# Attention scores of two heads in turn on the two halves of TensorE's rows, and forgetting-head values taken transposed on the halves of its columns

## The chip, the cores and the metric

One core of one Trainium2 chip. The metric is the device time of one execution in microseconds (us), of the slowest core, here the only one.

## The reference, cut to what matters

Two decoder layers over 256 tokens of width 1024, float32. Each has a token mixer, and after it a dense SwiGLU (layer 0) or a top-2-of-8 expert SwiGLU (layer 1); every sub-layer ends in a LayerNorm. The token mixer has two causal attention branches on one input projection:

```python
fq, fk, fv, fg, dq, dk, dv, ga, gb = jnp.split(u @ w_in, IN_SPLIT_POINTS, axis=-1)
# forgetting heads: 8 heads of 64, bias from a running sum of log-sigmoid gates
s = einsum('bqhd,bkhd->bhqk', fq, fk) * 64**-0.5 + cum_q - cum_k     # causal mask
y_fox = einsum('bhqk,bkhd->bqhd', softmax(s), fv)
# differential heads: 4 heads, two score maps each over 64, values of 128
s = einsum('bqhcd,bkhcd->bhcqk', dq, dk) * 64**-0.5 + rel_bias       # causal mask
p = softmax(s); a = p[:, :, 0] - lam * p[:, :, 1]
o = einsum('bhqk,bkhe->bqhe', a, dv)                                 # then an RMS norm per head
merged = sigmoid(ga) * (y_fox @ w_br_fox) + sigmoid(gb) * (y_diff @ w_br_diff)
mix = merged @ w_out
```

## The kernel before, in words

The queries lie in two blocks `t` of 128 tokens; block 0 sees 128 keys, block 1 sees 256 (`kw`). Large products run as pairs of reduced-precision parts (`whi`, `wlo` of a weight, `hTh`, `hTl` of the activations): `split` (L180 to L182) makes `whi` on ScalarE and `wlo` on VectorE from a loaded `raw`. Attention scores, transposes and values run in plain float32, for which TensorE makes two passes, each a weight load and a matmul.

`mixer` (L456 on) projects the forgetting values and gates, then `fq` and `fk`, and then runs two generators beside projections (`beside`, L506): `fox()`, the forgetting heads, beside the projections of `dk`, `dq` and `dv`; and `diff()`, the differential heads, beside those of the gates. The order of each engine's queue is not the order of the code: a scheduler puts the instructions in order when the program is built, by its own estimate of when each is ready.

`qk["fq"]` and its like hold two heads per 128-partition column block: the even head in partitions 0 to 63, the odd head in 64 to 127. A score product therefore contracts over 64 partitions and uses half of TensorE's rows.

`fox()` takes for each block the even heads, then the odd ones (`b`), in groups of four heads (block 0) or two (block 1). A group is one PSUM bank of tag `aux` (two buffers): the bias product `cum_RA,cum_L` and the mask product `maskb,identb` over all 128 rows, then one `fk,fq` product per head on half `b` of the rows; `softmax` (L435: one maximum on VectorE, one exponential per head on ScalarE); `blocks_T` (L448: four transposes, one copy by ScalarE); then per head and key block

```python
self.mm(o[:, h * 64:(h + 1) * 64], pT[:, blk * 128:(blk + 1) * 128],
        v["f", kb][:, h * 64:(h + 1) * 64], kb == 0, kb == t)
```

with tokens on `o`'s partitions: a weight load of 128 columns and a stream of 64. At the block's end VectorE divides `o` by the sums (L559), and `put_T` (L201) turns the result by four transposes and splits it into `yT`.

`diff()` has for each group the two maps `c` of a head in the two row halves; it does the bias products, the scores and the softmax of `c = 0` and then those of `c = 1`, normalises both on VectorE (L587, L588) and goes on as above, with values of 128 columns.

All matmuls are issued at L92 (`mm`). In the experts stage `plain_mm` (L977) already lets 2 or 4 products run on column halves or quarters of the array, one after the other by order-only dependencies; those are the products `aux<-raw,xs`.

Of the kernel before, what the change touches and what calls it, by code (L numbers as in the profile page):

```python
# [8 lines left out]
F32 = mybir.dt.float32  # L9
# [4 lines left out]
OP = mybir.AluOpType  # L14
# [43 lines left out]
class Body:  # L58
# [397 lines left out]
    def mixer(self, l, xT):  # L456
        nc, a, tc = self.nc, self.a, self.tc
        w = a["w_in"][l].rearrange("(k p) n -> p k n", p=128)
# [4 lines left out]
        v = {}  # L463
# [16 lines left out]
        qk = {}  # L480
# [36 lines left out]
        L, RA = self.forget(fg)  # L517
        yts = {}

        def y_tile():  # L520
            return self.at.tile([128, 512], F32, name="y", tag="y", bufs=2)

        def y_T(half):

            if half not in yts:
                yts[half] = [self.gran("yT", F32R) for _ in range(2)]
            return yts[half]

        def fox():
            for t in range(2):  # L530
                o = self.o_bank()
                si = self.at.tile([128, 8], F32, name="fsum", bufs=2)
                groups = [(b, 0, 4) for b in range(2)] if t == 0 else [(b, g, 2) for g in range(2) for b in range(2)]
                for b, g, n in groups:
                    heads = [b + 2 * (2 * g + i) for i in range(n)]
                    kw = 128 * (t + 1)
                    ps = self.aux_bank()
                    p3 = ps.rearrange("p (n w) -> p n w", w=kw)
                    h0 = heads[0]
                    self.mm(p3, L[:, t * 128:(t + 1) * 128], RA[b][:, 2 * g:2 * g + n, 0:kw], True, False)  # L540
                    self.mm(p3[:, :, kw - 128:kw], self.identb,
                            self.maskb[:, None, :].to_broadcast([128, n, 128]), False, False)
                    r0 = b * 64
                    for i in range(n):
                        jj = 2 * g + i
                        self.mm(p3[:, i], qk["fq"][r0:r0 + 64, jj, t * 128:(t + 1) * 128],
                                qk["fk"][r0:r0 + 64, jj, 0:kw], False, i == n - 1)
                    p, s = self.softmax(ps, n, kw, "p")
                    nc.vector.reciprocal(si[:, h0:h0 + 2 * n - 1:2], s[:, :n])
                    pT = self.blocks_T(p)  # L550
                    for i in range(n):
                        h = heads[i]
                        for kb in range(t + 1):
                            blk = i * (t + 1) + kb
                            self.mm(o[:, h * 64:(h + 1) * 64], pT[:, blk * 128:(blk + 1) * 128],
                                    v["f", kb][:, h * 64:(h + 1) * 64], kb == 0, kb == t)
                    yield
                yf = y_tile()
                nc.vector.tensor_tensor(yf.rearrange("p (h e) -> p h e", e=64),  # L559
                                        o.rearrange("p (h e) -> p h e", e=64),  # L560
                                        si[:, :, None].to_broadcast([128, 8, 64]), op=OP.mult)
                self.put_T(y_T(0), yf, t)

        def diff():
            for t in range(2):
                o = self.o_bank()
                kw = 128 * (t + 1)
                for g, n in ([(0, 4)] if t == 0 else [(0, 2), (2, 2)]):
                    pp = []
                    for c in range(2):  # L570
                        ps = self.aux_bank()
                        p3 = ps.rearrange("p (n w) -> p n w", w=kw)
                        for i, part in enumerate(self.bias):
                            self.mm(p3, self.antir, part[:, g:g + n, 256 - kw:256], i == 0, False)
                        for i in range(n):
                            self.mm(p3[:, i], qk["dq"][c * 64:c * 64 + 64, g + i, t * 128:(t + 1) * 128],
                                    qk["dk"][c * 64:c * 64 + 64, g + i, 0:kw], False, i == n - 1)
                        p, s = self.softmax(ps, n, kw, ("p", "p2")[c])
                        r = self.at.tile([128, 4], F32, name="sm_r", bufs=4)
                        nc.vector.reciprocal(r[:, :n], s[:, :n])  # L580
                        if c == 1:
                            nc.vector.tensor_scalar(r[:, :n], r[:, :n], lamn, None, op0=OP.mult)
                        pp.append((p, r))
                    (p1, r1), (p2, r2) = pp
                    for i in range(n):
                        cs = slice(i * kw, (i + 1) * kw)
                        nc.vector.tensor_scalar(p1[:, cs], p1[:, cs], r1[:, i:i + 1], None, op0=OP.mult)  # L587
                        nc.vector.scalar_tensor_tensor(p1[:, cs], p2[:, cs], r2[:, i:i + 1], p1[:, cs],  # L588
                                                       op0=OP.mult, op1=OP.add)
                    pT = self.blocks_T(p1)  # L590
                    for i in range(n):
                        h = g + i
                        for kb in range(t + 1):
                            blk = i * (t + 1) + kb
                            self.mm(o[:, h * 128:(h + 1) * 128], pT[:, blk * 128:(blk + 1) * 128],
                                    v["d", kb][:, h * 128:(h + 1) * 128], kb == 0, kb == t)
                    yield
                yd = y_tile()
                nc.scalar.activation(yd, o, AF.Square)
                ss = self.at.tile([128, 4], F32, name="ss", bufs=2)  # L600
                nc.vector.tensor_reduce(ss, yd.rearrange("p (h e) -> p h e", e=128), axis=AX, op=OP.add)
                nc.vector.tensor_scalar(ss, ss, 1.0 / 128.0, EPS, op0=OP.mult, op1=OP.add)
                rs = self.rsqrt(ss, 4)
                yd3 = yd.rearrange("p (h e) -> p h e", e=128)
                nc.vector.tensor_tensor(yd3, o.rearrange("p (h e) -> p h e", e=128),
                                        rs[:, :, None].to_broadcast([128, 4, 128]), op=OP.mult)
                nc.vector.tensor_tensor(yd3, yd3, sub[:, None, :].to_broadcast([128, 4, 128]), op=OP.mult)
                self.put_T(y_T(1), yd, t)
# [6 lines left out]
        def gating(i):  # L615
            for nm, c0 in (("a", C_GA), ("b", C_GB)):
# [5 lines left out]
                yield  # L622

        beside(fox(), (z for part in (proj("dk", C_DK, 1.0), proj("dq", C_DQ, 0.125), values()) for z in part), 0)
        beside(diff(), (z for i in range(4) for z in gating(i)), 0)

        if l == DEPTH - 1:
# [7 lines left out]
        for i in range(2):  # L635
            wpc = [self.piece(wb[j][:, :, 512 * i:512 * i + 512]) for j in range(2)]
            for jp in range(2):
                parts = []
                for br in range(2):
                    b = self.mm_bank()  # L640
                    for j in range(2):
# [3 lines left out]
                                                   op0=OP.add, op1=OP.mult)  # L645
# [3 lines left out]
                cs = slice(jp * 512, jp * 512 + 512)  # L649
                nc.scalar.activation(mt["h", i][:, cs], m, AF.Copy, scale=0.5)  # L650
                nc.vector.scalar_tensor_tensor(mt["l", i][:, cs], m, 0.5, mt["h", i][:, cs].bitcast(F32),
                                               op0=OP.mult, op1=OP.subtract)
# [786 lines left out]
```

## Time and profile before

| | |
|---|---|
| median of 3 runs | 1545.66 us (1544.31 to 1545.85) |
| profiled execution: its time, its span | 1546.93 us, 1545.2 us |
| TensorE busy (matmuls) | 1510.6 us, 98% |
| VectorE, ScalarE busy | 911.6 us (59%), 734.7 us (48%) |
| DMA, mean over the span | 294 GB/s |

Engines are named as in the profile: PE is TensorE's matmuls, PEld its weight loads, DVE VectorE, ACT ScalarE. A row of the order of time gives the start and the length of a group of equal instructions; a matmul's length takes in the time until its result has left the pipeline, so lengths of neighbours overlap, and the distance between starts tells what each costs the queue. A form such as `64*128 64x256` means a stationary operand of 64 rows and 128 columns and a moving one of 64 partitions and 256 columns.

### The profile page before, as it was taken

The numbers are of one execution on the slowest core, as the hardware profiler recorded it, in microseconds if no ns is written. First come the engines' busy times: TensorE is split into PE (matmuls) and PEld (weight loads), VectorE is DVE, ScalarE is ACT, GpSimd is POOL, SyncE is SP. The second block draws the span as 40 slices with busy tenths as digits, with TensorE's granted clock in tenths as the row PEclk, the third lists the DMA queues.
The fourth block names the chain that finished last, engine by engine and source line by source line (L and its number), as shares of the span: only waits on it lengthen the run. The fifth ranks groups of instructions, "written<-read, shape, count | busy, mean of one in ns | idle before, by whom it ended". The sixth has DMA issues, their size and how long they took to land. (4 is left out here: it accounts for less than half of the span.)

```text
span 1545.2 us, 24215 instructions
## 1 busy us (share of the span) xinstructions
PE 1510.6 (98%) x8798; PEld 1144.6 (74%) x8798; DVE 911.6 (59%) x1274; ACT 734.7 (48%) x1049; POOL 16.6 (1%) x43
## 2 busy tenths in 40 slices
PE   8999999999999999999999999999999999999996
PEld 6989979998798898666666566666666666666762
DVE  7546685545664657544535443766657576566774
ACT  4554444444365533254443333556555455555660
POOL 3000000000000000000000000000000000000000
PEclk9999999999999999999999999999999999999998
DMA  9633555555473340699999999999999999999993
GB/s 293 197 118 107 187 169 188 190 177 164 140 256 110 109 164 1 264 409 406 405 409 401 394 396 401 409 409 403 383 391 409 382 403 409 381 404 401 396 399 137
DMA packets 187347, 454.73 MB, mean 294 GB/s; under 512 B 13050, under 2 KB 68370, under 8 KB 187220
## 3 DMA queue, kind: packets, MB, share of 16 engines
q1 hardware_dynamic: 186432, 452.05, 77.9%
q0 software_dynamic: 784, 1.05, 0.5%
q8 instruction: 71, 1.16, 0.3%
q14 instruction: 56, 0.46, 0.1%
q10 hardware_dynamic: 4, 0.01, 0.0%
HBM read 452.00 MB, written 1.05 MB: 293 GB/s over the span
## 5 line engine op out<-in xcount | busy, mean ns | idle before, releaser
L182 DVE TENSOR_TENSOR wlo<-raw,whi 128x1024 fp32r<-128x1024 f32 (+2 forms) x524 | 617.2, 1202 | 370.1 <-ACT whi L181 365.4
L181 ACT ACTIVATE whi<-raw 128x1024 fp32r<-128x1024 f32 (+2 forms) x524 | 529.2, 1042 | 272.8 <-PE mm L92 168.6
L92 PE MATMUL mm<-hTh,wlo 128*128 128x256 f32 x672 | 192.2, 286 | 0.0
L92 PE MATMUL mm<-hTl,whi 128*128 128x256 f32 x672 | 191.8, 285 | 0.0
L92 PE MATMUL mm<-hTh,whi 128*128 128x256 f32 x672 | 191.1, 284 | 0.0
L92 PE MATMUL mm<-wlo,xh 128*128 128x512 f32 x448 | 179.8, 402 | 2.4 <-DVE wlo L182 2.0
L92 PE MATMUL mm<-whi,xl 128*128 128x512 f32 x448 | 175.1, 391 | 0.0
L92 PE MATMUL mm<-whi,eh 128*128 128x512 f32 x504 | 162.9, 398 | 0.6 <-ACT whi L181 0.6
L92 PE MATMUL aux<-raw,xs 128*32 128x512 f32 (+1 forms) x896 | 156.2, 598 | 0.0
L92 PE MATMUL mm<-whi,xh 128*128 128x512 f32 x448 | 154.6, 404 | 1.2 <-ACT whi L181 1.1
L92 PEld LDWEIGHTS mm<-hTh,wlo 128*128 128x128 f32 x672 | 128.5, 191 | 2.9 <-issue 2.0
L92 PEld LDWEIGHTS mm<-hTl,whi 128*128 128x128 f32 x672 | 128.7, 191 | 0.2
L92 PEld LDWEIGHTS mm<-hTh,whi 128*128 128x128 f32 x672 | 128.6, 191 | 0.2
L92 PEld LDWEIGHTS mm<-whi,eh 128*128 128x128 f32 x504 | 92.4, 188 | 38.0 <-ACT whi L181 9.6
L92 PEld LDWEIGHTS mm<-whi,xh 128*128 128x128 f32 x448 | 80.7, 188 | 46.7 <-issue 15.7
L92 PE MATMUL mm<-wlo,eh 128*128 128x512 f32 x280 | 107.9, 399 | 0.3
L92 PEld LDWEIGHTS mm<-wlo,xh 128*128 128x128 f32 x448 | 84.1, 188 | 25.4 <-DVE wlo L182 9.0
L92 PEld LDWEIGHTS aux<-raw,xs 128*32 128x32 f32 (+1 forms) x896 | 41.4, 123 | 82.0 <-issue 78.3
L1031 ACT ACTIVATE rows<-aux 128x512 f32<-128x512 f32 x56 | 33.3, 595 | 139.8 <-PE aux L92 139.8
L92 PEld LDWEIGHTS mm<-whi,xl 128*128 128x128 f32 x448 | 84.3, 188 | 16.8 <-issue 0.8
L92 PE MATMUL aux<-raw,eh 128*32 128x512 f32 (+1 forms) x448 | 78.7, 599 | 0.0
L92 PEld LDWEIGHTS mm<-wlo,eh 128*128 128x128 f32 x280 | 52.6, 188 | 12.1 <-DVE wlo L182 1.0
(323 smaller groups left out, 1976.4 us busy)
## 6 DMA issues: line engine op xcount, KB each, us to landing
raw<-in_w_expert_gate_up SPq DMA_DIRECT2D x448, 512.0 KB, 9.3
raw<-in_w_expert_down SPq DMA_DIRECT2D x224, 512.0 KB, 9.2
raw<-in_w_in SPq DMA_DIRECT2D x36, 1024.0 KB, 5.3
raw<-in_w_ffn_gate_up SPq DMA_DIRECT2D x22, 1024.0 KB, 5.0
raw<-in_w_ffn_down SPq DMA_DIRECT2D x10, 1024.0 KB, 4.9
raw<-in_w_out SPq DMA_DIRECT2D x8, 1024.0 KB, 5.0
raw<-in_w_in SPq DMA_DIRECT2D x8, 520.0 KB, 4.7
raw<-in_w_branch_fox SPq DMA_DIRECT2D x4, 1024.0 KB, 4.9
```

Source lines behind the costliest of these rows:

```text
L92: self.made = self.nc.tensor.matmul(out, lhsT, rhs, start=start, stop=stop)
L181: return (self.nc.scalar.activation(hi, src, AF.Copy), self.nc.vector.tensor_sub(lo, src, hi.bitcast(F32)))
L182: self.nc.vector.tensor_sub(lo, src, hi.bitcast(F32)))
L1031: self.nc.scalar.activation(r, bk, AF.Copy)
```

## The change

`fox()` and `diff()` now take both row halves of a group at once. A helper `in_turn` issues products that alternate between the two halves, each ordered behind the one before without a wait:

```diff
+        def in_turn(products):
+            made = []
+            for x in products:
+                self.mm(*x)
+                made.append(self.made.ins)
+            for x, y in zip(made, made[1:]):
+                self.behind(y, x, mybir.DependencyClass.NoSync)
```

In `fox()` the even and the odd heads of a group get a bank each, and both banks are filled before the softmax of either. The probabilities are divided by their sums on VectorE before they are transposed. The value product has its operands exchanged: the values (64 columns) are the stationary operand, the transposed probabilities (128 columns) stream, and the result is transposed already, with even heads on partitions 0 to 63 of `o` and odd heads on 64 to 127. So `o` is split straight into `yT`:

```diff
-                    self.mm(p3, L[:, t * 128:(t + 1) * 128], RA[b][:, 2 * g:2 * g + n, 0:kw], True, False)
...
-                    for i in range(n):
-                        jj = 2 * g + i
-                        self.mm(p3[:, i], qk["fq"][r0:r0 + 64, jj, t * 128:(t + 1) * 128],
-                                qk["fk"][r0:r0 + 64, jj, 0:kw], False, i == n - 1)
-                    p, s = self.softmax(ps, n, kw, "p")
-                    nc.vector.reciprocal(si[:, h0:h0 + 2 * n - 1:2], s[:, :n])
-                    pT = self.blocks_T(p)
...
-                nc.vector.tensor_tensor(yf.rearrange("p (h e) -> p h e", e=64),
-                                        o.rearrange("p (h e) -> p h e", e=64),
-                                        si[:, :, None].to_broadcast([128, 8, 64]), op=OP.mult)
-                self.put_T(y_T(0), yf, t)
+                    in_turn((p3[b][:, i], qk["fq"][rows[b], 2 * g + i, t * 128:(t + 1) * 128],
+                             qk["fk"][rows[b], 2 * g + i, 0:kw], False, i == n - 1) for i in range(n) for b in range(2))
+                    ps = []
+                    for b in range(2):
+                        p, s = self.softmax(p3[b].rearrange("p n w -> p (n w)"), n, kw, ("p", "p2")[b])
+                        r = self.at.tile([128, 4], F32, name="sm_r", bufs=4)
+                        nc.vector.reciprocal(r[:, :n], s[:, :n])
+                        for i in range(n):
+                            cs = slice(i * kw, (i + 1) * kw)
+                            nc.vector.tensor_scalar(p[:, cs], p[:, cs], r[:, i:i + 1], None, op0=OP.mult)
+                        ps.append(p)
                     yield
+                    pT = [self.blocks_T(p) for p in ps]
+                    in_turn((o[rows[b], (2 * g + i) * 128:(2 * g + i + 1) * 128],
+                             v["f", kb][:, (2 * (2 * g + i) + b) * 64:(2 * (2 * g + i) + b + 1) * 64],
+                             pT[b][:, (i * (t + 1) + kb) * 128:(i * (t + 1) + kb + 1) * 128], kb == 0, kb == t)
+                            for i in range(n) for kb in range(t + 1) for b in range(2))
+                    yield
+                cut = [p.rearrange("p (k s) -> p k s", s=256)[:, :, t * 128:(t + 1) * 128] for p in y_T(0)]
+                self.split(*cut, o.rearrange("p (k s) -> p k s", s=128))
```

In `diff()` the bias products of both maps come first, then the scores of all heads by `in_turn`, alternating between `c = 0` and `c = 1`, then both softmaxes; its values stay as they are.

Where the scheduler now puts the products: TensorE's queue at three places, the same in both layers. A row is one product of the code (two passes of the trace where it is float32), `x4` four in a row.

First, layer 0, block 0 of the forgetting heads. Before:

```order
L92 MATMUL aux<-cum_RA,cum_L 128x512
L92 LDWEIGHTS identb
L92 MATMUL aux<-maskb,identb 128x512
L92 MATMUL aux<-fk,fq 128x128 x4
L92 MATMUL mm<-hTh_157,whi 128x256
L92 MATMUL aux<-cum_RA,cum_L 128x512
L92 LDWEIGHTS identb
L92 MATMUL aux<-maskb,identb 128x512
L92 MATMUL aux<-fk,fq 128x128 x4
```

After the change:

```order
L92 MATMUL aux<-cum_RA,cum_L 128x512
L92 LDWEIGHTS identb
L92 MATMUL aux<-maskb,identb 128x512
L92 MATMUL aux<-fk,fq 128x128
L92 MATMUL mm<-hTh_157,whi 128x256
...
L92 MATMUL mm<-hTh_157,whi 128x256
L92 MATMUL aux<-cum_RA,cum_L 128x512
L92 LDWEIGHTS identb
L92 MATMUL aux<-maskb,identb 128x512
L92 MATMUL aux<-fk,fq 128x128 x7
```

The scheduler pulls the first even head ahead of the odd heads' bank, with seven projection matmuls between; the other seven products follow in one visit.

Second, layer 0, block 1 of the forgetting heads, the second group. Before, the two score visits and the values stand apart, of which this is the first score visit:

```order
L92 MATMUL aux<-cum_RA,cum_L 128x512
L92 LDWEIGHTS identb
L92 MATMUL aux<-maskb,identb 128x2x128
L92 MATMUL aux<-fk,fq 128x256 x2
L92 MATMUL mm<-whi,hTh_157 128x512
L92 MATMUL mm<-wlo,hTh_157 128x512
L92 MATMUL mm<-whi,hTl_159 128x512
L92 MATMUL mm<-whi,hTh_157 128x512
L92 MATMUL mm<-wlo,hTh_157 128x512
L92 MATMUL o<-fv,pT 128x64 x4
```

After the change:

```order
L92 MATMUL aux<-cum_RA,cum_L 128x512
L92 LDWEIGHTS identb
L92 MATMUL aux<-maskb,identb 128x2x128
L92 MATMUL aux<-cum_RA,cum_L 128x512
L92 LDWEIGHTS identb
L92 MATMUL aux<-maskb,identb 128x2x128
L92 MATMUL aux<-fk,fq 128x256 x2
L92 MATMUL o<-pT,fv 64x128 x7
L92 MATMUL aux<-fk,fq 128x256 x2
L92 MATMUL mm<-whi,hTh_157 128x512
```

Seven value products of the group before now stand inside the score visit; the eighth stands alone ahead of it.

Third, layer 0, block 0 of the differential heads. Before:

```order
L92 MATMUL aux<-bias_h,antir 128x512
L92 MATMUL aux<-bias_l,antir 128x512
L92 MATMUL aux<-dk,dq 128x128 x4
L92 MATMUL aux<-bias_h,antir 128x512
L92 MATMUL aux<-bias_l,antir 128x512
L92 MATMUL aux<-dk,dq 128x128 x4
L92 MATMUL mm<-hTh_157,wlo 128x256
```

After the change:

```order
L92 MATMUL aux<-bias_h,antir 128x512
L92 MATMUL aux<-bias_l,antir 128x512
L92 MATMUL aux<-bias_h,antir 128x512
L92 MATMUL aux<-bias_l,antir 128x512
L92 MATMUL aux<-dk,dq 128x128 x8
L92 MATMUL mm<-hTh_157,wlo 128x256
```

Two visits became one of eight products. Elsewhere in a layer the score products now come, in this order, as 1, 2 and 1 (block 1 of the forgetting heads, first group), as 2 and 2 (above), and as 1, 3 and 4 (block 1 of the differential heads); before they came as 1, 1, 1, 1, 2, 2 and 2, 2, 2, 2. The value products of the forgetting heads come as 1, 7, 1, 7 and 8. The queues of SyncE and GpSimd, which issue the DMAs, read the same in both kernels.

## Rows read from the trace of the kernel before

**Rows 1.** Stretches 66:140 and 463:537: us, busy by engine, PEclk, DMA share, GB/s

```profile
66.00:140.00 74.00, 74.00 (x497) 63.22 (x496) 38.63 (x78) 38.60 (x96) 0.00 (x0) 1.00 0.36 114
463.00:537.00 74.00, 74.00 (x496) 63.22 (x495) 38.71 (x77) 38.68 (x96) 0.21 (x1) 1.00 0.36 114
```

**Rows 2.** Order of time, PE, 66.6 to 68.4: start us, us, engine line op

```profile
66.68 0.39 PE L92 MATMUL aux<-maskb,identb 128*128 128x512 bf16 x1
67.00 1.16 PE L92 MATMUL aux<-fk,fq 64*128 64x128 f32 x8
...
68.31 0.40 PE L92 MATMUL aux<-cum_RA,cum_L 128*128 128x512 f32 x1
```

**Rows 3.** Order of time, PE, 93.0 to 96.9

```profile
93.09 0.28 PE L92 MATMUL aux<-maskb,identb 128*128 128x256 bf16 x1
93.31 1.13 PE L92 MATMUL aux<-fk,fq 64*128 64x256 f32 x4
...
94.95 0.40 PE L92 MATMUL mm<-whi,hTl 128*128 128x512 f32 x1
95.18 0.40 PE L92 MATMUL mm<-whi,hTh 128*128 128x512 f32 x1
...
95.65 1.00 PE L92 MATMUL o<-fv,pT 128*128 128x64 f32 x8
...
96.77 0.39 PE L92 MATMUL mm<-whi,hTh 128*128 128x512 f32 x1
```

**Rows 4.** Order of time, PE, 73.5 to 75.7

```profile
73.60 0.28 PE L92 MATMUL aux<-maskb,identb 128*128 128x256 bf16 x1
73.81 0.70 PE L92 MATMUL aux<-fk,fq 64*128 64x256 f32 x2
...
74.69 0.70 PE L92 MATMUL aux<-fk,fq 64*128 64x256 f32 x2
...
75.61 0.27 PE L451 MATMUL tp<-ident,p 128*128 128x128 f32 x1
```

**Rows 5.** Order of time, PE, 117.6 to 118.4

```profile
117.65 0.60 PE L205 MATMUL tp<-ident,y 128*128 128x128 f32 x4
...
118.21 0.28 PE L92 MATMUL mm<-hTh,wlo 128*128 128x256 f32 x1
118.33 0.28 PE L92 MATMUL mm<-hTh,whi 128*128 128x256 f32 x1
```

**Rows 6.** Order of time, PE and then PEld, 980 to 985 (experts, column halves)

```profile
980.24 3.65 PE L92 MATMUL aux<-raw,xs 128*64 128x512 f32 x16
983.83 1.20 PE L92 MATMUL tp<-y,back 128*128 128x512 f32 x4
984.87 0.40 PE L92 MATMUL mm<-whi,xh 128*128 128x512 f32 x1
...
980.24 0.20 PEld L92 LDWEIGHTS aux<-raw,xs 128*64 128x64 f32 x4 [0.37 <-PE tp L92]
980.73 0.14 PEld L92 LDWEIGHTS aux<-raw,xs 128*64 128x64 f32 x2 [0.29 <-issue]
981.15 0.14 PEld L92 LDWEIGHTS aux<-raw,xs 128*64 128x64 f32 x2 [0.29 <-issue]
981.58 0.14 PEld L92 LDWEIGHTS aux<-raw,xs 128*64 128x64 f32 x2 [0.29 <-issue]
```

**Rows 7.** Groups by line and form, 66 to 140: line engine op xcount | busy us, mean ns | idle

```profile
L440 DVE TENSOR_REDUCE sm_m<-aux 128x4 f32<-128x512 f32 x4 | 2.8, 692 | 3.6 <-PE aux L92 3.6
L587 DVE TENSOR_SCALAR p<-p,sm_r 128x256 f32<-128x256 f32 x4 | 1.2, 350 | 0.0
L587 DVE TENSOR_SCALAR p<-p,sm_r 128x128 f32<-128x128 f32 x4 | 0.9, 282 | 0.0
...
L444 ACT ACTIVATION_READ_ACCUMULATOR p<-aux,sm_m 128x1 f32 x32 | 6.4, 200 | 0.0
L444 ACT ACTIVATE p<-aux,sm_m 128x128 f32<-128x128 f32 x16 | 5.7, 366 | 3.5 <-DVE sm_m L440 3.1 <-issue 0.4
```

More of the change, by code (lines that the diff above doesn't have):

```diff
@@ L531, in fox @@
                 o = self.o_bank()
[L532 to L539, printed above, removed]
-                    self.mm(p3, L[:, t * 128:(t + 1) * 128], RA[b][:, 2 * g:2 * g + n, 0:kw], True, False)
-                    self.mm(p3[:, :, kw - 128:kw], self.identb,
-                            self.maskb[:, None, :].to_broadcast([128, n, 128]), False, False)
-                    r0 = b * 64
-                    for i in range(n):
-                        jj = 2 * g + i
-                        self.mm(p3[:, i], qk["fq"][r0:r0 + 64, jj, t * 128:(t + 1) * 128],
-                                qk["fk"][r0:r0 + 64, jj, 0:kw], False, i == n - 1)
-                    p, s = self.softmax(ps, n, kw, "p")
-                    nc.vector.reciprocal(si[:, h0:h0 + 2 * n - 1:2], s[:, :n])
-                    pT = self.blocks_T(p)
[L551 to L556, printed above, removed]
-                    yield
@@ L558, in fox @@
-                yf = y_tile()
-                nc.vector.tensor_tensor(yf.rearrange("p (h e) -> p h e", e=64),
-                                        o.rearrange("p (h e) -> p h e", e=64),
-                                        si[:, :, None].to_broadcast([128, 8, 64]), op=OP.mult)
-                self.put_T(y_T(0), yf, t)
+                kw = 128 * (t + 1)
+                n = 4 // (t + 1)
+                for g in range(t + 1):
+                    p3 = []
+                    for b in range(2):
+                        ps = self.aux_bank()
+                        p3.append(ps.rearrange("p (n w) -> p n w", w=kw))
+                        self.mm(p3[b], L[:, t * 128:(t + 1) * 128], RA[b][:, 2 * g:2 * g + n, 0:kw], True, False)
+                        self.mm(p3[b][:, :, kw - 128:kw], self.identb,
+                                self.maskb[:, None, :].to_broadcast([128, n, 128]), False, False)
+                    rows = [slice(b * 64, b * 64 + 64) for b in range(2)]
+                    in_turn((p3[b][:, i], qk["fq"][rows[b], 2 * g + i, t * 128:(t + 1) * 128],
+                             qk["fk"][rows[b], 2 * g + i, 0:kw], False, i == n - 1) for i in range(n) for b in range(2))
+                    ps = []
+                    for b in range(2):
+                        p, s = self.softmax(p3[b].rearrange("p n w -> p (n w)"), n, kw, ("p", "p2")[b])
[5 more added lines that the diff above has]
+                        ps.append(p)
+                    yield
+                    pT = [self.blocks_T(p) for p in ps]
[4 more added lines that the diff above has]
+                    yield
@@ L569, in diff @@
                     pp = []
+                    p3 = []
                     for c in range(2):
-                        ps = self.aux_bank()
-                        p3 = ps.rearrange("p (n w) -> p n w", w=kw)
+                        p3.append(self.aux_bank().rearrange("p (n w) -> p n w", w=kw))
                         for i, part in enumerate(self.bias):
[L574 to L578, printed above, removed]
+                            self.mm(p3[c], self.antir, part[:, g:g + n, 256 - kw:256], i == 0, False)
+                    in_turn((p3[c][:, i], qk["dq"][c * 64:c * 64 + 64, g + i, t * 128:(t + 1) * 128],
+                             qk["dk"][c * 64:c * 64 + 64, g + i, 0:kw], False, i == n - 1) for i in range(n) for c in range(2))
+                    for c in range(2):
+                        p, s = self.softmax(p3[c].rearrange("p n w -> p (n w)"), n, kw, ("p", "p2")[c])
                         r = self.at.tile([128, 4], F32, name="sm_r", bufs=4)
```

## The prediction

> **What bounds the kernel now.** I read the page's first part (engine shares), then the stretches of the two attention stages, then the order of time of TensorE inside them. The busy shares of the page are means over stages, so the stretch matters: in 66 to 140 us (attention of layer 0) and 463 to 537 us (layer 1) TensorE is busy 74.00 of 74.00 us at full granted clock, VectorE and ScalarE some 38.6 each, and the DMA engines 36% [rows 1]. The two layers read alike. So here a microsecond off TensorE's queue is a microsecond off the program, as long as nothing that feeds it comes late: the FFN follows on TensorE too, and the expert weights are fetched only once the router has chosen, so their stream starts earlier by the same amount.
>
> A busy figure counts matmuls that merely stand in the pipeline, so I price by the distance between starts. A float32 product is two passes, each a weight load and a matmul, and the trace counts passes.
>
> Prices. A full matmul of 256 columns takes 0.12 from start to start, one of 512 takes 0.23 [rows 3, 5]. A score visit of four heads at 128 columns (8 passes): from the mask's start at 66.68 to 68.31 are 1.63; less the mask as a 512-column matmul (0.23) and one 256-column matmul (0.12) leaves **1.28** [rows 2]. A visit of two heads at 256 columns (4 passes): 93.09 to 95.18 are 2.09; less a 256-column mask (0.12) and three matmuls of 512 (0.69) leaves **1.28** again [rows 3]. A visit with one head between two transposes: 73.60 to 75.61 are 2.01; less mask 0.12, two transposes 0.22 and a matmul 0.12 leaves 1.55 for two, **0.78** each [rows 4]. Four transposes: 117.65 to 118.33 are 0.68, less two matmuls, 0.11 each [rows 5].
>
> Inside a visit a pass is its stream. In the experts stage two column halves run together and a round of both starts every 0.42 to 0.43 for 512 columns [rows 6], so 0.11 for 128 and 0.215 for 256. Then the 8 passes of 0.11 leave 0.40 of their 1.28, and the 4 of 0.215 leave 0.42: **a visit to half the rows costs 0.41 beside its stream**, lost on the way in and on the way out. The tempting reading is that loads are exposed on every pass and that alternating would hide them. Of the 256-column row, 4 passes last 1.13 with the last one's drain [rows 3]; at 0.215 plus an exposed 0.11 they would last 1.3 before any drain. They are hidden already, and the gain can come only from streams that run at once.
>
> A visit to the column halves: 980.24 to 983.83 are 3.59 for 8 rounds, 0.15 over 8 x 0.43; the next four 512-column matmuls take 1.04 against 0.92, 0.12 more [rows 6]; the way in I take as at 93.09 to 93.31, 0.22 for a matmul of 0.12, so 0.10 [rows 3]. Together **0.37**.
>
> **The change, part by part (per layer).**
> Scores. Before there are 14 visits: ten of 1.28 (four at 128 columns, six with two heads of 256) and four of 0.78, 15.92 in all. After, by the order of the built program, the scheduler does not keep the alternating products together; the visits are: 1 head at 128 columns (2 x 0.11 + 0.41 = 0.63); 7 at 128 (three pairs of heads and one alone, 8 rounds, 0.88 + 0.41 = 1.29); 8 at 128 (8 rounds, 1.29); one head at 256 three times (2.34); 2 at 256 (2 rounds, 0.84); 2 + 2 at 256 around seven value products (4 rounds, 1.27); 3 at 256 (4 rounds, since one head has no partner, 1.27); 4 at 256 (4 rounds, 1.27). Sum 10.20, gain **5.72**. This supposes that halves of rows overlap as halves of columns do, which no row here shows for rows. Of the ends (no overlap, full overlap) I take full: the column rows are the nearest, and the passes alternate in the same way there. Its other end is a rival.
>
> Values. Before: 48 passes of 64 columns, eight in 95.65 to 96.77 less a 0.23 matmul, 0.89, 0.111 each [rows 3]; such a pass streams 64 columns and is bound by its 128-column weight load. 48 x 0.111 = 5.33. After: 48 passes of 128 columns on column halves, in five visits, of 1, 7, 1, 7 and 8 products: 2 x (0.22 + 0.37) + 3 x (0.88 + 0.37) = 4.93, the one inside the score visit charged as a visit of its own. Gain **0.40** only: what pairing gives, the new visits nearly eat.
>
> Transposes. y of the forgetting heads is no longer turned: 8 x 0.11 = **0.88**.
>
> Off TensorE. VectorE gets 16 normalisations, 8 of 128 columns at 0.28 and 8 of 256 at 0.35 [rows 7], 5.0 us, and loses the division of o. VectorE has 35 us free of 74 [rows 1], so I cost it at nothing; with no cover it would be 5.0 a layer, 10 in all. ScalarE's and VectorE's splits of y stay and read o's bank instead of tp's. DMA queues are unchanged.
>
> New wait. Both aux banks are now filled before either softmax, so the next pair needs both emptied. At 128 columns that is one maximum 0.69 and eight exponentials of 0.37 + 0.20 [rows 7], 5.3; behind the seven-head visit 46 matmuls of 0.12 stand, 5.5, and the first bank, asked for first, is free at 3.0. Hidden, though not by much.
>
> **Sum.** 5.72 + 0.40 + 0.88 = 7.0 per layer, 14.0 for two. The profiled execution took 1546.93, so it would take 1532.9; the median of the three runs is 1.3 lower, 1545.66, which gives 1531.7. I say **1532**.
>
> **Rivals.**
> *Loads of the two row halves go one after the other.* A 128-column load costs about a pass of 0.111 (the value passes above). Then 128-column rounds gain nothing: the visits of 7 and 8 heads cost 14 x 0.11 + 0.41 = 1.95 and 16 x 0.11 + 0.41 = 2.17, 1.54 more; at 256 columns two loads (0.22) just fit a round. Plus 3.1: **1535**. For it: the halves of columns share 128 columns of weights, the halves of rows need 128 each. Against: four 64-column loads there took 0.20 together, where a row of two takes 0.14 [rows 6].
> The Trainium skill (TensorE: Matmul & The Clock Gate, LDWEIGHTS) says that a load's time goes by its columns and not by its rows, which speaks for this rival. The same page (Measured speedup vs the span model) has four row tiles 3.07 times as fast as one, short of four; by that ratio as an estimate a pair gains 1.54 and not 2, and my sum would end at 1534; the paired column rows here reach 2, so I keep 2.
>
> *The row halves do not overlap at all*, so that the change does not do what it says. Added to my sum are 0.66 and 0.88 (visits of 7 and 8), 0.43 (2 at 256), 0.86 (2 + 2), 0.43 (3) and 0.86 (4), 4.12 per layer: **1540**. For it: no row shows two row halves at once, and both write all 128 partitions. Against: they write different banks.
>
> *A wait takes the gain: slower.* At each of the six pairs of a layer the second bank's softmax is what the next pair or the transposes wait for. If its four exponentials (2.28 at 128 columns) lay bare at all 12 pairs, 27.4 would be lost: **1559**. It decides above (14.0 + 3.1) / 12 = 1.4 a pair. For it: the first reserve is 0.2. Against: TensorE waits nowhere in these stretches now [rows 1], and later pairs have more products between.
> *The same, at two or three places only*, 4 us in all: **1536**.
>
> **How the numbers follow.** Full overlap 0.58; loads in turn or a partial overlap 0.20; no overlap 0.13; a few waits 0.05; waits everywhere 0.04. A measurement tells 0.2% (3.1 us) from no change. The first four are all faster by more than that; I leave 0.03 for no overlap together with waits, which ends as the same, and 0.04 for slower, so 0.93 for faster. The range: below, if the value visits cost nothing on the way in and out, 5 x 0.37 x 2 = 3.7 less, 1528; above, no overlap and a microsecond, 1541. Only the waits lie outside.
>
> **What would show it.** Right: the 16 passes of the eight-head visit at 128 columns in about 1.1 us from first to last start with starts in pairs; the eight at 256 in about 1.1 too; seven value products in 1.0; half as many transposes of y; both attention stretches some 7.0 us shorter with TensorE still full. Loads in turn: pairs at 256 columns but 128-column passes still 0.11 apart. No overlap: 256-column passes still 0.215 apart. Waits: gaps ahead of transposes of p or of the score's first matmul, ended by ScalarE or VectorE. I would be wrong altogether if the stretches shrank and a later stage gave it back, for which I see no place.

## The result and the profile after

| | before | after |
|---|---|---|
| median, runs on one chip (6 each) | 1545.12 us (1544.31 to 1548.94) | **1535.24 us** (1533.05 to 1536.12) |
| profiled execution, its span | 1546.93, 1545.2 | 1533.21, 1531.5 |
| TensorE busy (matmuls) | 1510.6 | 1494.3 |
| VectorE, ScalarE busy | 911.6, 734.7 | 917.5, 735.6 |

After over before is **0.9927** (95% interval 0.9913 to 0.9941), so 11.3 us faster (9.1 to 13.4); the two medians lie 9.9 apart, inside that interval. Forecast were 14.0, and 1532. The sign and the place were right; the size is 2.7 short by the ratio. The two profiled executions lie 13.7 apart; that this comes so near to 14.0 is luck, as the sum at the end of this section shows.

First the stretches of the attention stages of the profile after (columns as in [rows 1]), which answer to [rows 1]:

```profile
66.00:133.00 67.00, 67.00 (x497) 57.46 (x497) 42.99 (x92) 40.56 (x98) 0.00 (x0) 1.00 0.40 125
457.00:524.00 67.00, 67.00 (x496) 57.34 (x495) 42.77 (x92) 40.55 (x98) 0.21 (x1) 1.00 0.40 125
```

As many matmuls as filled 74.00 us, 497 and 496, fill 67.00 now, with TensorE busy throughout at full granted clock: no wait took the gain. To measure it exactly I take two marks, the first `cum_RA,cum_L` product and the last transposes of y, in the order of time of TensorE. Before, layer 0 and layer 1:

```profile
66.44 0.40 PE L92 MATMUL aux<-cum_RA,cum_L 128*128 128x512 f32 x1
159.58 0.38 PE L205 MATMUL tp<-ident,y 128*128 128x128 f32 x2
...
463.52 0.40 PE L92 MATMUL aux<-cum_RA,cum_L 128*128 128x512 f32 x1
556.67 0.38 PE L205 MATMUL tp<-ident,y 128*128 128x128 f32 x2
```

After:

```profile
63.78 0.40 PE L92 MATMUL aux<-cum_RA,cum_L 128*128 128x512 f32 x1
152.55 0.38 PE L205 MATMUL tp<-ident,y 128*128 128x128 f32 x2
...
454.98 0.40 PE L92 MATMUL aux<-cum_RA,cum_L 128*128 128x512 f32 x1
543.75 0.38 PE L205 MATMUL tp<-ident,y 128*128 128x128 f32 x2
```

From mark to mark it was 93.14 and is 88.77, 4.37 less, in both layers alike. But more projection products lie between the marks now. The groups by line and form between the marks of layer 0 (count behind the x), before:

```profile
L92 PE MATMUL mm<-hTh,wlo 128*128 128x256 f32 x134 | 38.8, 289 | 0.0
L92 PE MATMUL mm<-hTl,whi 128*128 128x256 f32 x134 | 38.7, 289 | 0.0
L92 PE MATMUL mm<-hTh,whi 128*128 128x256 f32 x134 | 38.4, 286 | 0.0
```

After:

```profile
L92 PE MATMUL mm<-hTh,wlo 128*128 128x256 f32 x142 | 41.1, 289 | 0.0
L92 PE MATMUL mm<-hTh,whi 128*128 128x256 f32 x142 | 40.8, 288 | 0.0
L92 PE MATMUL mm<-hTl,whi 128*128 128x256 f32 x142 | 40.5, 285 | 0.0
```

24 more of 256 columns, at 0.12 each 2.88, which the stretch behind the marks no longer has to do. So the change itself takes 4.37 + 2.88 = **7.25 a layer**, where 7.0 was forecast. In the same way, marks less 0.12 per projection product, the experiments below are compared, as "attention per layer" against before and after.

Next the visits (a visit is an unbroken run of products on half the rows or half the columns), in the order of time of TensorE after:

```profile
66.24 1.16 PE L92 MATMUL aux<-fk,fq 64*128 64x128 f32 x14
67.33 0.39 PE L92 MATMUL mm<-hTl,whi 128*128 128x256 f32 x1
...
81.26 1.09 PE L92 MATMUL o<-pT,fv 128*64 128x128 f32 x14
...
105.21 1.16 PE L92 MATMUL aux<-dk,dq 64*128 64x128 f32 x16
106.31 0.39 PE L92 MATMUL mm<-hTh,wlo 128*128 128x256 f32 x1
...
123.23 1.14 PE L92 MATMUL aux<-dk,dq 64*128 64x256 f32 x8
124.29 0.39 PE L92 MATMUL mm<-hTh,wlo 128*128 128x256 f32 x1
```

Sixteen passes of 128 columns take the 1.16 that eight took [rows 2]; eight of 256 take 1.14 where four took 1.13 [rows 3]. The starts come in pairs 6 to 7 ns apart, a round every 0.112 us at 128 columns and 0.216 at 256. Seven value products on the column halves (14 passes) last 1.09. That is full overlap of the row halves, loads included.

What the end gave back stands in the order of time of VectorE, with the idle time ahead and what ended it in brackets. Before, behind the branch on the count of tokens that found no room in their expert:

```profile
1533.11 1.28 DVE L250 BATCH_NORM_STATS2 ln_st<-acc 128x6 f32<-128x512 f32 x2
1534.65 0.28 DVE L256 BATCH_NORM_AGGREGATE ln_mv<-ln_st 128x2 f32<-128x12 f32 x2 [0.27 <-DVEq L1286]
```

After:

```profile
1517.08 1.27 DVE L250 BATCH_NORM_STATS2 ln_st<-acc 128x6 f32<-128x512 f32 x2
1520.93 0.28 DVE L256 BATCH_NORM_AGGREGATE ln_mv<-ln_st 128x2 f32<-128x12 f32 x2 [2.58 <-DVEq L1295]
```

The same two operations, in code that the change does not touch, now have **2.58** between them in place of 0.27. TensorE is through by then, and from the second operation to the end of the span it is 10.6 us in both, so all 2.31 lie on the path.

The third part of the difference is TensorE's granted clock (last but two in a row of stretches). Before:

```profile
20.00:30.00 10.00, 7.98 (x43) 7.62 (x44) 6.24 (x14) 3.83 (x6) 2.16 (x4) 0.66 1.04 320
205.00:225.00 20.00, 17.34 (x88) 13.76 (x87) 17.39 (x36) 8.73 (x10) 0.00 (x0) 1.00 0.41 131
```

After:

```profile
20.00:30.00 10.00, 7.91 (x65) 7.70 (x66) 8.74 (x17) 6.39 (x10) 2.16 (x4) 1.00 1.08 332
205.00:225.00 20.00, 17.09 (x100) 14.76 (x99) 16.38 (x37) 8.56 (x12) 0.00 (x0) 0.83 0.63 210
```

In each stretch that stands below 1.00, TensorE ran 6.83 us at the lower of its two levels: before from 21.7, after from 211.9 (before also 3.41 at 646.3). TensorE has waited just ahead of both places, at the start and for the LayerNorm between the sub-layers, in both kernels. The start cost before 2.66 (66.44 against 63.78 at the first mark); the piece at 211.9 cost after some 1.4, by the distance from the marks of layer 0 to those of layer 1; for the piece at 646.3 the sum leaves 0.2. All of it for the profiled pair: attention 14.5, the clock 1.5 net, the end -2.3, together 13.7. The clock, with which the prediction did not reckon, gave back two thirds of what the end took.

### The profile page after: what moved, and what is told of

It reads as the page before. It is cut to its first block, busy times and chain, and to the rows that moved or that the text cites. A ratio compares the mean times of both kernels' runs of the same rounds, so it can differ in the third digit from the quotient of the medians.

```text
span 1531.5 us, 24214 instructions
## 1 busy us (share of the span) xinstructions
PE 1494.3 (98%) x8782; PEld 1129.4 (74%) x8782; DVE 917.5 (60%) x1302; ACT 735.6 (48%) x1049; POOL 16.8 (1%) x43
## 3 DMA queue, kind: packets, MB, share of 16 engines
q8 instruction: 71, 1.16, 0.3%
## 5 line engine op out<-in xcount | busy, mean ns | idle before, releaser
L92 PEld LDWEIGHTS mm<-wlo,eh 128*128 128x128 f32 x280 | 52.6, 188 | 12.2 <-DVE wlo L182 0.9
```

Source lines behind the costliest of these rows:

```text
L92: self.made = self.nc.tensor.matmul(out, lhsT, rhs, start=start, stop=stop)
```

## The experiments

All times are medians beside runs of the kernel before on the same chip, whose medians were 1546.80 (e1 to e4), 1546.24 (e5 to e8) and 1546.94 (e9 to e12). "End" is the idle time of VectorE ahead of the aggregate shown above.

| run | median | ratio (95%) | attention per layer against after | end |
|---|---|---|---|---|
| e1, the change again | 1535.08 | 0.9928 (0.9914 to 0.9941) | 0.00 | 2.54 |
| e2, rows in sequence | 1536.84 | 0.9940 (0.9926 to 0.9954) | +1.83 | 2.54 |
| e3, visits kept | 1527.11 | 0.9883 (0.9868 to 0.9898) | -3.68 | 2.72 |
| e4, before with small operations | 1549.32 | 1.0020 (1.0011 to 1.0029) | +7.29 | 2.62 |
| e5, halves apart | 1545.01 | 0.9994 (0.9984 to 1.0004) | +5.86 | 2.81 |
| e6, forgetting heads only | 1542.22 | 0.9971 (0.9958 to 0.9983) | +3.30 | 2.54 |
| e7, differential heads only | 1540.66 | 0.9963 (0.9949 to 0.9978) | +5.41 | 0.27 |
| e8, division twice | 1535.08 | 0.9929 (0.9913 to 0.9946) | +0.06 | 2.58 |
| e9, visits kept, one division | 1525.38 | 0.9860 (0.9843 to 0.9876) | -3.74 | 0.27 |
| e10, one division everywhere | 1525.28 | 0.9859 (0.9842 to 0.9875) | -3.74 | 0.27 |
| e11, visits kept, again | 1527.58 | 0.9870 (0.9854 to 0.9887) | -3.68 | 2.54 |
| e12, columns in sequence | 1536.84 | 0.9938 (0.9921 to 0.9954) | +1.83 | 2.53 |

Before is +7.24 in the column on attention. An end of 0.27 is called short below, one of 2.5 and more long. Counted from the branch to the next instruction of VectorE of any kind, the wait is 0.58 where the end is short and 2.84 to 3.12 where it is long.

**e1, the change again.** The kernel after as it is, beside e2 to e4.

> The changed kernel once more. In its trace the two attention stages are 7.2 us shorter each than before (first score bias to last transpose of y, allowing for the 24 projection matmuls that the scheduler moved), yet its median stood only 9.9 us below the median of before. Theory A: 14 to 14.5 us are won in the attention stages in every run, and some 2.3 are given back in every run at the end, where VectorE waits 2.9 us after the branch on the overflow count against 0.6 before; what is left of the difference is where the clock's half-speed stretches fall. It then expects the 2.9 us wait again, the same attention stages, and 10 to 13 us below before. Rival: the wait at the end is chance and absent this time; then 13 to 15 below before.

Measured 1535.08; from mark to mark, in projections and in the end it is as in the first profile. Only the pieces at the lower clock lie otherwise: three of 3.41, at 22.8, 214.0 and 630.4. The attention gain and the end belong to the kernel; the clock is the execution's.

**e2, rows in sequence.** The scores of a group are issued first for one half, then for the other, in `fox()` and `diff()`:

```diff
-  ... for i in range(n) for b in range(2))
+  ... for b in range(2) for i in range(n))
```

> The changed kernel with the score products issued half by half (all heads of one row half, then all of the other) instead of in turn. By the prices of the prediction its score visits cost 14.0 us a layer against 10.2, its six value visits 5.5 against 4.9, so 4.4 a layer and 8.8 in all: 1544, almost all of the gain gone. In the trace 128-column passes 0.11 apart and 256-column passes 0.215 apart, one by one, but for one pair where the first half ends and the second begins. Rival: if the gain came from fewer visits and the dropped transposes rather than from alternation, this stays within 3 us of the changed kernel.

Measured 1536.84, +1.83 a layer: three quarters of the gain in attention (5.41 of 7.24) stay, against the expectation of 4.4 a layer lost. By its number the rival came true, 1.8 us slower than e1; the rows give another reason, and e5 decides. The order of time of TensorE in e2:

```profile
91.91 1.14 PE L92 MATMUL aux<-fk,fq 64*128 64x256 f32 x8
92.98 0.50 PE L92 MATMUL mm<-whi,hTh 128*128 128x512 f32 x1
...
107.73 1.71 PE L92 MATMUL aux<-dk,dq 64*128 64x128 f32 x16
109.37 0.39 PE L92 MATMUL mm<-hTh,wlo 128*128 128x256 f32 x1
```

Two products of one half and then two of the other last 1.14, like those issued in turn; their starts come in pairs 13 ns apart. Four and then four (107.73) last 1.71, between the 1.16 of products in turn and 2.04 without any pairing (1.16 and eight passes of 0.11 more); three pairs lie in the middle. So TensorE itself starts a product of the other half while it stands close behind in the queue. The Trainium skill (TensorE: Matmul & The Clock Gate, The mechanism, under "What overlaps and what doesn't") says that matmuls start strictly in program order; the starts at 91.91 do not look like that. Part of the 1.83 is the scheduler's: in e2 it gave the two halves of the first group a visit each.

**e3, visits kept.** The products of a group are kept in one visit, scores behind the second bank's mask or bias, values behind the copy of the second `pT`:

```diff
+            with tc.high_priority():
...
+            if last is not None:
+                self.behind(made[0], last, kind)
```

> The changed kernel with the products of each pair kept in one visit: the first score product stands behind the second bank's bias or mask, the first value product behind the second copy of transposed probabilities, and the first differential scores behind the last forgetting values. The visits are then 8, 4, 4 and 8, 4, 4 score products and 8, 8, 8 value products a layer. By the prices (0.41 and 0.37 a visit beside the stream) the score visits cost 7.7 against 10.2 and the value visits 3.75 against 4.9, 3.7 less a layer, 7.4 in all: 1528. Rival: the products now wait for the later of two banks, and TensorE with them; then no gain over the changed kernel, or a loss.

Measured 1527.11, -3.68 a layer. The order of time of TensorE at the first group: all eight heads in one visit,

```profile
65.72 1.16 PE L92 MATMUL aux<-fk,fq 64*128 64x128 f32 x16
66.81 0.39 PE L92 MATMUL mm<-hTh,whi 128*128 128x256 f32 x1
```

as long as the visit of seven at 66.24 after, and the lone product at 64.33 is gone. The price of a visit (0.41 and 0.37) holds, and what the scheduler splits costs 3.7 a layer.

**e4, before with small operations.** 26 operations on eight numbers per partition are put on VectorE of the kernel before, whose result is overwritten:

```diff
+                for k in range(PAD[t]):
+                    nc.vector.tensor_scalar(si, bf, 1.0, None, op0=OP.mult)
```

> The kernel before with 26 small VectorE instructions of some 0.06 us (8 columns each, their result unused) in the attention stages, which puts the branch on VectorE at the same place in its instruction stream as in the changed kernel. Theory A, in its form that the place of the branch decides the wait: 2.9 us instead of 0.6 after the branch, 2.3 us slower than before. Rival: the wait has another cause; then 0.6 and the time of before.

Measured 1.0020 (1.0011 to 1.0029), so 1.7 to 4.5 us slower than before, with attention as before (+7.29 against +7.24). The order of time of VectorE at the end of e4:

```profile
1537.62 1.28 DVE L251 BATCH_NORM_STATS2 ln_st<-acc 128x6 f32<-128x512 f32 x2
1541.52 0.28 DVE L257 BATCH_NORM_AGGREGATE ln_mv<-ln_st 128x2 f32<-128x12 f32 x2 [2.62 <-DVEq L1289]
```

The long wait appears with nothing of the change in the kernel. It goes with the number of instructions that VectorE's queue has had by the branch: 1760 before (short), 1786 here and 1785 after (long), counted in the trace, waits on semaphores included.

**e5, halves apart.** The changed kernel, values and division too, but each bank's scores follow directly on its own bias:

```diff
+                        for i in range(n):
+                            self.mm(p3[b][:, i], qk["fq"][rows[b], 2 * g + i, t * 128:(t + 1) * 128],
...
-                    in_turn((p3[b][:, i], qk["fq"][rows[b], 2 * g + i, t * 128:(t + 1) * 128],
```

> Half by half in one visit lost only 1.8 us, and its trace shows why: where four products of the one half and then four of the other stand in the queue, or two and two, passes of the two halves start together all the same. So here the halves are put in visits of their own, as before the change: bias, mask or bias and scores of one bank, then those of the other; values, division and transposes as in the changed kernel. Theory B (the gain is that streams of two halves run at once, in whatever order they are issued, as long as they stand in one visit): score visits 15.6 a layer and value visits 5.5, together 21.2 against 15.1 in the changed kernel: 12 us slower than it, 1547, no gain left although the transposes are dropped. Rival: the gain came from values, transposes or something else; then under 5 us slower than the changed kernel.

Measured 1545.01, no different from before, +5.86 a layer. The order of time of TensorE at the first group, two visits as in [rows 2]:

```profile
65.65 1.16 PE L92 MATMUL aux<-fk,fq 64*128 64x128 f32 x8
66.74 0.38 PE L92 MATMUL mm<-hTh,whi 128*128 128x256 f32 x1
...
67.51 1.16 PE L92 MATMUL aux<-fk,fq 64*128 64x128 f32 x8
```

By the prices of the prediction the score visits of e5 cost 5.4 more than after, and a sixth value visit that the scheduler splits off 0.6: 6.0, where 5.86 were measured. So the gain needs both halves within one visit. What e5 still has over before is 7.24 - 5.86 = 1.4 a layer, 2.8 in all, and the end takes 2.5 of it.

**e6 and e7, one kind of heads alone.** In e6 `diff()` is that of before, in e7 `fox()` is.

> The changed forgetting heads with the differential heads as before. The differential score visits are 8.0 a layer instead of 4.6: 6.7 slower than the changed kernel, 1542; the wait at the end 2.9 as in the changed kernel, since VectorE's branch stands at nearly the same place.

> The changed differential heads with the forgetting heads as before. Its differential visits are one of 8 products, four of one and one of 4, 5.7 a layer against 7.7 before: 4.0 faster than before in the attention stages. VectorE's branch stands where it stood before, so theory A expects the wait at the end to be 0.6 again, and the time 4 below before: 1541 to 1542. Rival: the long wait comes with any change of the kernel; then 2.3 more.

Attention per layer: e6 is 3.30 over after, so 3.94 under before; e7 is 1.83 under before. Together they give 5.77 of the 7.24: the scheduler splits the visits otherwise in each (in e7 the four scores of one group of `diff()` come one by one). e7 has 1760 instructions ahead of the branch, as before, and keeps the short end (0.27); e6 has 1783 and the long one. By attention and end alone e6 would be 1.9 ahead of e7 (2 x 2.11 less 2.3); by the medians it is 1.6 behind, but its profiled execution had 13.6 us at the lower clock and that of e7 6.8. These medians do not rank the two; the stretches do.

**e8, division twice.** Each division of p by its sum is followed by a multiplication by 1.0:

```diff
+                            nc.vector.tensor_scalar(p[:, cs], p[:, cs], 1.0, None, op0=OP.mult)
```

> The changed kernel with each of VectorE's 16 divisions a layer followed by a multiplication by one: 5.0 us more work for VectorE a layer, at a place where the transposes wait for it. If the new division is hidden, as the prediction has it, the attention stages stay within 0.5 us a layer of those of the changed kernel (its visits, which the scheduler arranges anew, come to 15.4 a layer against 15.1). Rival: it lies on TensorE's path; then up to 5 a layer, 10 in all, slower. The branch on VectorE stands 33 instructions later than in the changed kernel: whether the wait after it is long there too tells how it hangs on the place.

Measured 1535.08, +0.06 a layer. The added work on VectorE is hidden.

**e9 to e11, towards a better version.** e9 is e3 with one operation for all heads of a bank; e10 does the same for the first map in `diff()`; e11 is e3 once more, beside them.

```diff
-                        for i in range(n):
-                            cs = slice(i * kw, (i + 1) * kw)
-                            nc.vector.tensor_scalar(p[:, cs], p[:, cs], r[:, i:i + 1], None, op0=OP.mult)
+                        pw = p.rearrange("p (n w) -> p n w", w=kw)
+                        nc.vector.tensor_tensor(pw, pw, r[:, :n, None].to_broadcast([128, n, kw]), op=OP.mult)
```

> The kernel with visits kept, and the new division of the forgetting heads as one VectorE instruction for all heads of a bank instead of one a head: 20 VectorE instructions less, so that the branch stands 5 behind its place in the kernel before (1765 against 1760). TensorE's order is the same in its visits (8, 4, 4, 8, 4, 4 and 8, 8, 8), so 1527 if the wait at the end stays at 3.0, and 1525 if it falls back to 0.6. It has been long at 1782 and short at 1760: the theory of the place leaves both open here.

> As the run above, and the first map's division of the differential heads in one instruction too: the branch stands at 1755, ahead of its place in the kernel before. Theory of the place: 0.6 us after the branch, and with the visits kept 2.4 below the kernel with visits kept, 1524.7. Rival: the wait is long in every kernel whose forgetting heads are changed; then 3.0 and 1527.

> The kernel with visits kept once more, beside the two above on one chip: 1527, wait at the end 3.0, attention stages as in its first run.

e9 and e10 take 1525.38 and 1525.28, e11 1527.58. Attention is the same in the three to 0.06; what differs is the end. With 1765 and 1755 instructions ahead of the branch instead of 1786 it is short again, in the order of time of VectorE of e9:

```profile
1513.09 0.28 DVE L256 BATCH_NORM_AGGREGATE ln_mv<-ln_st 128x2 f32<-128x12 f32 x2 [0.27 <-DVEq L1302]
```

These are the fastest kernels of the study, 21.6 and 21.7 under before, about twice the gain of the change.

**e12, columns in sequence.** The value products first for the even heads, then for the odd ones:

```diff
-                            for i in range(n) for kb in range(t + 1) for b in range(2))
+                            for b in range(2) for i in range(n) for kb in range(t + 1))
```

> The changed kernel with the value products half by half. The scheduler then puts them in visits of 4, 4, 4, 4 (one column half each) and 8 (four of one half, then four of the other): 1.25 each for the first four, and for the last between 1.25 and 2.13, by how many of its passes TensorE pairs of its own accord. With three pairs, as the score visit of 8 showed in the half-by-half run, 1.8; together 6.8 a layer against 4.9: 1.9 a layer and 3.8 in all slower than the changed kernel, 1539. Rival: value products are bound by weight loads and not by their stream; then no difference.

Measured 1536.84 and +1.83 a layer. The order of time of TensorE in e12:

```profile
80.04 1.09 PE L92 MATMUL o<-pT,fv 128*64 128x128 f32 x8
81.06 0.39 PE L92 MATMUL mm<-hTh,wlo 128*128 128x256 f32 x1
...
106.35 1.58 PE L92 MATMUL o<-pT,fv 128*64 128x128 f32 x16
107.86 0.50 PE L92 MATMUL aux<-bias_l,antir 128*128 128x512 f32 x1
```

Four products of one half (8 passes) last the 1.09 that seven of both halves (14) last in the kernel after: alone they start 0.109 apart, the time of their stream of 128 columns, since their load has 64 now. The value passes of before were 0.111 apart, with a load of 128 columns and a stream of 64. So the exchange of operands makes a pass no cheaper; the pairs do. Where four and four stand together (106.35), TensorE pairs some of them.

## Why the prediction was right, and where it was not

**What bounds it.** Right: TensorE is full in both stretches before and after, and as many matmuls take 67.00 for 74.00.

**Scores, 5.72 a layer.** Right. e5, which gives this up and has a value visit more, loses 5.86; by the prices 0.59 of that is the value visit, and its score visits cost 0.28 less than those of before, so the scores are worth an estimated 5.55. Full overlap, taken from the column halves, holds for the row halves: rounds of 0.112 and 0.216 where 0.11 and 0.215 were taken. The rival of loads in turn falls with the 128-column visits (1.16 for 16 passes, not 2.17), and that of no overlap with those of 256 columns. The Trainium skill (TensorE: Matmul & The Clock Gate, Measured speedup vs the span model) has four row tiles at 3.07 times one and no figure for two; the 1.54 for a pair that the prediction estimated from it does not come out here, where a pair takes the time of one, to a few ns.

**Values and transposes, 0.40 + 0.88.** Forecast 1.28 together; the 7.25 leave an estimated 1.7 beside the scores. They were not measured apart.

**The price of a visit, 0.41 and 0.37.** Right: e3 takes the scheduler's splits out and gains the 3.7 a layer that these prices give.

**VectorE's division at nothing.** Right for the attention stage, by e8.

**No new wait in attention.** Right: TensorE is busy 67.00 of 67.00. The rivals with waits fall.

**The sum.** 14.0 forecast, 14.5 in the trace, 11.3 (9.1 to 13.4) by the ratio. **The step that failed is VectorE's division "at nothing", and with it "a later stage gave it back, for which I see no place".** The place is the branch behind the experts. The division costs nothing where it stands, but it adds instructions to VectorE's queue (1785 ahead of the branch, not 1760), and with that the wait behind the branch is 2.3 longer; e4 brings it about in the kernel before, and e9, with fewer instructions for the same division, takes it away from e3. 14.5 less 2.3 is 12.2, inside the interval. The 0.9 between 12.2 and 11.3 is not settled: the pieces at the lower clock move an execution by 1 to 3 us. The medians scatter as much: 9.9 apart in the first comparison, 11.7 in that of e1, which has the same kernel.

**Why the wait depends on the count** was not shown by a run; what VectorE waits for, the traces indicate. The wait is short at 1755, 1760 and 1765 instructions and long at 1782 to 1786 and at 1818. The Trainium skill (Runtime: NRT & Kernel Launch, Instruction fetch mechanics) says that a taken branch to a target outside the pages that an engine holds has to fetch the page first; a place in the queue that decides would fit that. The times of the packets of instructions fit it too. The first row gives the DMA share in 40 slices of the 3.1 us from the branch on, with a digit in the slice in which a packet starts; then come the DMA queues (packets, MB, share). Before:

```profile
DMA  0000000000000040000000000006000000000000
q8 instruction: 1, 0.02, 1.7%
q14 instruction: 1, 0.01, 1.1%
```

After:

```profile
DMA  0000000000000300000000000000000900000000
q8 instruction: 1, 0.02, 2.4%
q14 instruction: 1, 0.01, 0.9%
```

One packet of each kind follows the branch in either kernel, 1.2 us (q14) and 2.2 us (q8) behind it before and 1.0 and 2.5 after. But VectorE goes on in the 8th slice before, ahead of both, and in the 37th after the change, behind both. So it is in every run: in the ten with the long wait a q14 packet starts 1.0 to 1.3 us behind the branch and VectorE goes on 1.8 to 1.9 us after that; in the four with the short wait no packet of instructions starts before VectorE goes on, and the first comes 0.6 us later. ScalarE takes the same branch 3.5 us earlier and waits 2.5 to 2.7 us in all fourteen, with a q14 packet 0.9 to 1.2 us behind its branch. This speaks for a fetch of instructions that the short waits are spared; it is argued from the order in time. Why the count decides stays open: no run moved the branch's target while keeping the count.

## What to carry to other kernels

Of two products that use the two halves of TensorE's rows or columns, the second costs next to nothing, but only inside one visit, so put them together first and then see that the scheduler leaves them together: here its splits cost 3.7 a layer, half as much as the change won in attention. And what an edit adds to an engine with time to spare is free only up to the next place where that engine's instruction stream itself matters: count the instructions ahead of a branch, and look at the wait behind it in the profile after.

## What the runs showed of the hardware

- Two halves of the rows overlap in full, loads of 128 columns included: 0.112 us a pair at 128 columns and 0.216 at 256 (after).
- TensorE starts a product of the other half before earlier ones of the same half, if it stands close behind (e2: pairs 13 ns apart with two and two, three pairs with four and four).
- The wait behind a taken branch was 0.58 us in four profiled executions and 2.84 to 3.12 in ten, by the number of VectorE instructions ahead of it. A packet of instructions starts inside the long wait, and none inside the short one.
- Pieces of 3.41 or 6.83 us at the lower clock level come at some of the places where TensorE has just waited, in one execution and not in another of the same kernel: e3 has 6.83 at 208.1, e11 3.41 at 23.3 and 3.41 at 624.0. e11 reaches the first mark 1.62 later, as it would if half of 3.41 were lost.
